# Rows turned between output halves, a second state buffer, and the first output weights converted behind three blocks' decayed scores of the last scan

## The chip, the cores and the metric

The kernel runs on one core of a Trainium2 chip. Its engines each have their own queue of instructions and run beside each other: TensorE (PE, with its weight loads PEld), VectorE (DVE), ScalarE (ACT), GpSimd (POOL) and SyncE (SP), whose queue issues most of the DMAs. The metric is device time in microseconds, the median of several executions. The profile records one execution in detail.

## The reference

One step of a hybrid diffusion backbone with one layer: 128 context tokens and 1024 latent tokens of width 1024. Each layer norms and modulates its input, projects it once, and feeds two groups of heads side by side: grouped-query attention (8 query heads of 64) and a bidirectional mLSTM (4 heads of 128), a scan over chunks of 128 tokens in both directions. Both are merged by one output projection, and a gated feed-forward net of width 2816 follows.

```python
def trunk_layer(x, mods, ...):
    h = rmsnorm(x, norm1_w) * (1 + sc1) + sh1
    aq, ak, av, mq, mk, mv, mo, mg = jnp.split(h @ w_in, SPLIT_POINTS, axis=-1)
    attn_o = attention(aq, keys, vals)
    hm, st_f, st_b = mlstm_bidir(heads(mq), heads(mk) * (MLSTM_DK ** -0.5), heads(mv), gates, init_f, init_b)
    hm = rmsnorm(hm.transpose(0, 2, 1, 3), mlstm_norm_w.reshape(MLSTM_HEADS, MLSTM_DV))
    hm = (hm.reshape(B, T, MLSTM_WIDTH) * jax.nn.sigmoid(mo.astype(F32))).astype(x.dtype)
    mix = jnp.concatenate([attn_o, hm], axis=-1) @ w_out
    x = x + g1 * mix
    h2 = rmsnorm(x, norm2_w) * (1 + sc2) + sh2
    x = x + g2 * swiglu(h2, w_gu, w_down)
```

Inside the scan, the step for one chunk:

```python
    s = jnp.einsum('bhld,bhsd->bhls', qc, kc) * jnp.exp(log_d - m_t[..., None])
    num = jnp.einsum('bhls,bhse->bhle', s, vc) + inter[..., None] * jnp.einsum('bhld,bhde->bhle', qc, C)
    h = num / jnp.maximum(jnp.abs(den), jnp.exp(-m_t))[..., None]
    C_new = decay[..., None, None] * C + jnp.einsum('bhs,bhsd,bhse->bhde', w, kc, vc)
```

## The kernel before

The 1152 tokens are nine blocks of 128 rows (block 0 is the context), in three groups of three. Products that need full precision are made from a high and a low part of each operand: ACT rounds a tile to its high part (a CAST, L157 for weights), DVE or POOL subtracts it from the full tile (L137) to get the low part, and PE makes three products, high by high, high by low and low by high. So each weight piece of 128x1024 costs one cast and one subtraction.

The order of the instructions on each engine is not written out by hand. The program is written as generators that are woven together, and the scheduler of the Tile framework places what they emit on the engines by its own timeline, within limits: `tc.high_priority` moves a piece forward, and `tc.issue_after(x)` places what follows behind instruction x in that order, without a semaphore of its own. Buffers come from pools with a tag and a count; a new tile of a tag waits until the oldest one has been read for the last time.

The stages that matter here:

The heads. `head_project(h)` makes the projections of mLSTM head h and, block by block, the state contributions; `head_mlstm(h)` is the scan of that head. Projection h runs woven with scan h - 1. Each head loads two initial states, forward (tag `c0f`, two buffers) and backward (tag `c0b`, one buffer): L807 and L808 on SP's queue. The states between blocks are tiles of tag `cs`, 21 buffers. The backward states are joined by seven steps in a row on DVE (L862), the first of which reads the backward initial state.

The last scan (head 3) has no projection beside it. For each block `weights(b)` makes a score product (L875), a decay in PSUM (L877, L878), two exponentials on ACT (`dt`, L881) and the decayed scores on DVE (`sd`, L883). Three blocks are made ahead. Then come the products with the states (L898), the evacuation `it` (L901), the products with the values (L905), and the normalisation on DVE, ACT and POOL. Beside this scan runs `attn_out_first`: the attention half of the output projection for blocks 0 to 2. It loads pieces of `w_out` into `ip` tiles, converts them to `ir` tiles (L157 on ACT, L137 on DVE), converts the attention output to `mxa` (L1310 on ACT, L137 on POOL) and makes twelve products for each block and each half of 512 columns (L1183 to L1185, here called output products). Products L364 for the remaining modulation also run there.

`prefill` comes next. It adds the mLSTM half of the output projection to the nine row blocks. For each block, `mix(b)` turns the block's 128 rows by four transposes (`hmr`, L116), casts them (`mx`, L1227) and subtracts (L137); `half(b, n)` makes twelve output products for one half of the columns and adds the gated result (DVE L1144, POOL L1145; for blocks 6 to 8 L1243 and L1244, with the row kept in DRAM); `end(b)` takes sums of squares (L1345) and starts the second norm (`y`, L1361). Blocks 0 and 1 are turned together ahead of the rest. Into this the attention of the second group of blocks is woven: for each head scores S on PE (L1075, one buffer of three PSUM banks), the row maximum on DVE (L1077), exponentials on ACT (`pr`, L1078), the scaled halves `ph` (ACT, L1081) and `pl` (DVE, L1082), transposes by DMA (L1084, L1085) and the products with the values (L1099, L1100).

Then the feed-forward net follows for the three groups, with gate and up products (L1382 to L1384) and down products (L1155 to L1157).

Of the kernel before, what the change touches and what calls it, by code (L numbers as in the profile page):

```python
# [8 lines left out]
F32 = mybir.dt.float32  # L9
# [4 lines left out]
AF = mybir.ActivationFunctionType  # L14
# [5 lines left out]
P = 128  # L20
# [17 lines left out]
LAST = [(0, 5), (5, 5), (10, 4), (14, 4), (18, 4)]  # L38
PAIRS = [(0, 1), (2, 3), (4,), (5, 6), (7, 8)]
NG = 4  # L40
CSB = 21
SINGLES = [(b,) for b in range(NB)]


# [1 line left out]
def hybrid_step(ctx: ExitStack, tc: tile.TileContext, I: dict, O: dict):  # L46
# [11 lines left out]
    def nm(s):  # L58
        uid[0] += 1
        return f"{s}_{uid[0]}"  # L60
# [57 lines left out]
    def bc(ap, axis, shape):  # L118
        return ap.unsqueeze(axis).to_broadcast(shape)
# [430 lines left out]
    for tag, shape, bufs, dt in (("hm", [P, NB, P], 2, F32), ("ssh", [P, NB], 2, F32), ("nu", [P, 2, P + 1], 4, F32), ("it", [P, 2, P + 1], 3, F32),  # L550
                                 ("dn", [P, 2], 3, F32), ("jkh", [P, P], 1, BF16), ("sd", [P, 2, P], 4, F32), ("dt", [P, 2, P], 4, F32),
                                 ("so", [P, P], 9, F32), ("va", [P, P + 1], 9, F32), ("kT", [P, P], 9, F32), ("th", [P, P], 1, F32),
                                 ("kt", [P, P], 2, F32), ("wv", [P, 2, P + 1], 2, F32), ("c0f", [P, P + 1], 2, F32), ("c0b", [P, P + 1], 1, F32),
                                 ("cs", [P, P + 1], CSB, F32), ("qTm", [P, CT], 2 * NCH, F32)):
        mlp.tile(shape, dt, name=f"lay_{tag}", tag=tag, bufs=bufs)

# [211 lines left out]
    def qcol(i, d, b, h):  # L768
        c = d * 64 + b * 4 + h
        return QT[:, i, c : c + 1]  # L770
# [3 lines left out]
    def head_project(h, st):  # L774
# [28 lines left out]
        st["s"] = states = {}  # L803
        st["raw"] = raws = {}
        for d in range(2):
            c0 = mlp.tile([P, P + 1], F32, name=nm("c0"), tag=("c0f", "c0b")[d], bufs=2 - d)
            dma(c0[:, 0:P], I["state_C"][0, 0, d, h])  # L807
            dma(c0[:, P : P + 1], I["state_n"][0, 0, d, h].rearrange("(p o) -> p o", o=1))  # L808
            states[d, 1 if d == 0 else NBL] = c0
# [47 lines left out]
    def head_mlstm(h, st):  # L857
# [14 lines left out]
        def weights(b):  # L872
            qTb = st["q"][b // CB][:, b % CB * P : (b % CB + 1) * P]
            pd = bank()
            mm(pd[:, 0:P], blocks[b][0], qTb, start=True, stop=True)  # L875
            r = b * 4 + h
            mm(pd[:, P : 3 * P], identb, maskb.rearrange("p d l -> p (d l)"), start=True, stop=False)  # L877
            mm(pd[:, P : 3 * P], selb[:, r : r + 1].to_broadcast([P, P]), NM3.rearrange("p d l -> p (d l)"), start=False, stop=True)  # L878
            dt = mlp.tile([P, 2, P], F32, name=nm("dt"), tag="dt", bufs=4)
            for d in range(2):  # L880
                act(dt[:, d], pd[:, (d + 1) * P : (d + 2) * P], AF.Exp, bias=qcol(0, d, b, h))  # L881
            sd = mlp.tile([P, 2, P], F32, name=nm("sd"), tag="sd", bufs=4)
            dve.tensor_tensor(out=sd, in0=bc(pd[:, 0:P], 1, [P, 2, P]), in1=dt, op=ALU.mult)  # L883
            return qTb, sd

        ahead = [weights(b) for b in range(depth)]
# [301 lines left out]
    def prefill(cur, nxt):  # L1188
# [16 lines left out]
        def load_x1(b):  # L1205
            if CB <= b < 2 * CB:
                dma(x1s[1][b % CB], xrow(b))
# [49 lines left out]
        for b in range(2):  # L1257
            half(b, 0)
            yield
        for b in range(2):  # L1260
            load_x1(b + 2)
            half(b, 1)
            yield
            yield from end(b)
        for b in range(2, NB):
            load_x1(b + 2)
            mix(b)
            yield
            for n in range(2):
                half(b, n)  # L1270
                yield
            yield from end(b)

    def attn_out_first(oT, ready):
# [18 lines left out]
        def out():  # L1293
            for n in range(2):
                cs = slice(n * 512, (n + 1) * 512)
                ws = []
                for j in range(2):
                    rows = w_out[2 * j * P : (2 * j + 2) * P, cs].rearrange("(a p) n -> p a n", p=P)
                    with tc.issue_after(sts[-1]["act"].ins), tc.issue_after(sts[-1]["dve"].ins):
                        ws.append(load_piece([(full_view, rows)], (2, 512), raw=raws[j], own=(his[j], los[j])))  # L1300
                for cnd in range(2):
                    dma(gt[:, 2 * n + cnd], g_d[0, cnd : cnd + 1, cs].to_broadcast([P, 512]))
                yield
                for i in range(CB):
                    while i not in ready:
                        yield
                    th, tl = mx[:, i, 0:4], mx[:, i, 4:8]
                    if n == 0:
                        dma(x1[:, i], xrow(i))
                        nc.scalar.copy(th, oT[i])  # L1310
                        sub(tl, oT[i], th.bitcast(F32), "pool")
                        yield
                    ps = out_block([ws], 0, th, tl)
                    v = x1[:, i, cs]
                    dve.tensor_tensor(out=gt[:, 4], in0=ps, in1=gt[:, 2 * n + (i > 0)], op=ALU.mult)
                    pool.tensor_tensor(out=v, in0=v, in1=gt[:, 4], op=ALU.add)
                    yield
# [310 lines left out]
```

## Time and profile before

| what | us |
|---|---|
| runs, median of 3 | 1536.48 |
| runs, lowest and highest | 1536.39, 1541.33 |
| profiled execution, its own time | 1540.57 |
| profiled execution, span from first to last instruction | 1538.8 |
| PE busy | 1479.7 |
| DVE busy | 1019.1 |
| ACT busy | 771.3 |
| POOL busy | 272.3 |

The last scan starts at about 446 us of the span, `prefill` at 490, and the first gate product of the feed-forward net at 577. From 600 to 880 us and from 920 to 1240, PE is shown busy all the time.

In a line of the timeline stand the start in us, the duration in us, the engine, the line of the kernel, the operation, the tiles written and read with their sizes, how many instructions are merged, and in brackets how long the engine idled before and what ended it. Matmuls overlap, so their durations add up to more than the time that they take. The clock is the share of full TensorE speed that was granted.

### The profile page before, as it was taken

The page shows a single profiled execution, that of the slowest core. Times are in us where ns is not written, and L with a number is a line of the kernel's source. Part 1 is how long each engine was busy: PE and PEld are TensorE (multiplying, and loading weights), DVE is VectorE, ACT ScalarE, POOL GpSimd, SP SyncE. Part 2 cuts the span into 40 slices and gives each one's busy share as a digit, 9 for nine tenths or more (in the row PEclk, how much of TensorE's full clock was granted, in tenths as well). Part 3 has the DMA queues.
Part 4 walks back from the last instruction along what each step waited for, and adds up shares of the span by engine and source line. Part 5 has one row for each costly group of instructions (what it writes and reads, how often), then busy time and mean ns, then how long its engine had stood idle before and what let it go on. Part 6 is the DMA issues. An engine that isn't in the chain of part 4 may idle for free.

```text
span 1538.8 us, 23409 instructions
## 1 busy us (share of the span) xinstructions
PE 1479.7 (96%) x8539; PEld 1245.3 (81%) x8539; DVE 1019.1 (66%) x2025; ACT 771.3 (50%) x1429; POOL 272.3 (18%) x354
## 2 busy tenths in 40 slices
PE   6799999999989899999999999999999999999997
PEld 3545567677766679899898989989898989999996
DVE  4878654838657875878646497887856584554554
ACT  4764475847654544555332445556553443333333
POOL 0112423233434441010010101000010101101110
PEclk9799999999999999999999999999999999999998
DMA  9664323523365566978634457877754445544441
GB/s 359 191 203 148 100 71 42 119 52 66 75 212 167 156 145 193 214 152 199 170 123 149 152 154 239 188 175 175 181 135 143 145 155 160 157 131 137 141 142 60
DMA packets 387113, 233.77 MB, mean 152 GB/s; under 512 B 170102, under 2 KB 347462, under 8 KB 386998
## 3 DMA queue, kind: packets, MB, share of 16 engines
q1 hardware_dynamic: 385006, 228.69, 54.0%
q10 hardware_dynamic: 1864, 3.20, 1.1%
q8 instruction: 67, 1.10, 0.3%
q14 instruction: 48, 0.39, 0.1%
q0 software_dynamic: 128, 0.39, 0.1%
HBM read 182.21 MB, written 11.69 MB: 126 GB/s over the span
## 4 chain that ended last, share of the span: by engine, by line
PE 58%; DVE 3%; DMA 1%; ACT 1%; issue 0%; ACTq 0%
PE mm L1383 12%; PE mm L1384 12%; PE mm L1382 12%; PE mm L1155 5%; PE mm L1156 5%; PE mm L1157 5%; PE S L1075 3%; PE po L1099 1%; PE po L1100 1%; PE mm L1185 1%; PE mm L1184 1%; PE mm L1183 1%; DVE fl L1371 1%; DVE wlo L137 1%; DVE t L1144 0%; DVE x L1145 0%
## 5 line engine op out<-in xcount | busy, mean ns | idle before, releaser
L157 ACT CAST whi<-raw 128x1024 fp32r<-128x1024 f32 (+1 forms) x216 | 221.8, 1027 | 390.3 <-PE mm L1383 151.5
L137 DVE TENSOR_TENSOR wlo<-raw,whi 128x1024 fp32r<-128x1024 f32 (+1 forms) x216 | 260.4, 1205 | 183.4 <-ACT whi L157 182.8
L1383 PE MATMUL mm<-aTl,whi 128*128 128x384 f32 x1056 | 355.9, 337 | 2.7 <-DVE aTl L137 2.7
L1384 PE MATMUL mm<-aTh,wlo 128*128 128x384 f32 x1056 | 354.1, 335 | 0.0
L1382 PE MATMUL mm<-aTh,whi 128*128 128x384 f32 x1056 | 352.5, 335 | 0.0
L137 POOL TENSOR_TENSOR hl<-tn,hl 128x384 fp32r<-128x384 f32 x66 | 85.3, 1292 | 848.7 <-ACT hl L1405 713.8
L1383 PEld LDWEIGHTS mm<-aTl,whi 128*128 128x128 f32 x1056 | 198.4, 188 | 3.9 <-DVE aTl L137 3.3
L1384 PEld LDWEIGHTS mm<-aTh,wlo 128*128 128x128 f32 x1056 | 198.4, 188 | 0.1
L1382 PEld LDWEIGHTS mm<-aTh,whi 128*128 128x128 f32 x1056 | 198.0, 188 | 0.6
L1156 PE MATMUL mm<-wlo,hl 128*128 128x512 f32 x372 | 145.3, 391 | 0.0
L1155 PE MATMUL mm<-whi,hl 128*128 128x512 f32 x372 | 144.1, 392 | 0.0
L1157 PE MATMUL mm<-whi,hl 128*128 128x512 f32 x372 | 142.6, 392 | 0.0
L1082 DVE SCALAR_TENSOR_TENSOR pl<-pr,st,ph 128x1152 f16<-128x1152 f32 (+1 forms) x72 | 96.0, 1334 | 33.0 <-ACT ph L1081 32.9
L1078 ACT ACTIVATE pr<-S,st 128x1152 f32<-128x1152 f32 (+1 forms) x72 | 81.2, 1128 | 34.5 <-DVE st L1077 33.9
L1077 DVE TENSOR_REDUCE st<-S 128x1 f32<-128x1152 f32 (+1 forms) x72 | 88.9, 1235 | 13.6 <-PE S L1075 12.9
L1081 ACT ACTIVATE ph<-pr,st 128x1152 f16<-128x1152 f32 (+1 forms) x72 | 83.8, 1164 | 20.9 <-DVE st L1080 8.0
L506 PE MATMUL wi<-headw,hT 128*128 128x384 f16 x288 | 93.9, 326 | 0.2 <-ACT th L792 0.2
L508 PE MATMUL wi<-headw,hT 128*128 128x384 f16 x288 | 93.9, 326 | 0.0
L507 PE MATMUL wi<-headw,hT 128*128 128x384 f16 x288 | 93.9, 326 | 0.0
L1144 DVE TENSOR_TENSOR t<-mm,gl 128x512 f32<-128x512 f32 x102 | 68.8, 685 | 27.5 <-DMA gl<-g_d 12.2
L1075 PE MATMUL S<-kst,qT 128*128 128x384 f32 (+1 forms) x400 | 84.4, 344 | 2.4 <-ACT pr L1078 2.4
L1157 PEld LDWEIGHTS mm<-whi,hl 128*128 128x128 f32 x372 | 69.9, 188 | 14.4
(396 smaller groups left out, 2647.7 us busy)
## 6 DMA issues: line engine op xcount, KB each, us to landing
raw<-in_w_gu_dram SPq DMA_DIRECT2D x132, 512.0 KB
raw<-in_w_down_dram SPq DMA_DIRECT2D x60, 512.0 KB
a<-in_w_ada_dram SPq DMA_DIRECT2D x24, 512.0 KB
gl<-g_d SPq DMA_DIRECT2D x36, 256.0 KB
aw<-in_w_ada_dram SPq DMA_DIRECT2D x16, 512.0 KB
iraw<-in_w_in_dram SPq DMA_DIRECT2D x32, 256.0 KB
raw<-in_w_out_dram SPq DMA_DIRECT2D x12, 512.0 KB
x<-in_x_sample_dram SPq DMA_DIRECT2D x11, 512.0 KB
```

The lines of the kernel that those rows point to most:

```text
L137: (dve if eng == "dve" else pool).tensor_tensor(out=out, in0=full, in1=hi, op=ALU.subtract)
L157: nc.scalar.copy(hi[:, :n], raw[:, :n])
L506: mm(ps[:, :n], ah, wh[:, k % 2, c0 : c0 + n], start=(k == 0), stop=False)
L507: mm(ps[:, :n], ah, wl[:, k % 2, c0 : c0 + n], start=False, stop=False)
L1075: mm(S[:, n, 0:w], qT[:, h, :], kst[kv][:, t, c0 + n * w : c0 + (n + 1) * w], start=(t == 0), stop=(t == 1))
L1082: dve.scalar_tensor_tensor(out=plv, in0=prv, scalar=st[:, 3:4], in1=phv, op0=ALU.mult, op1=ALU.subtract)
L1155: mm(ps, ah, wh[:, k % 2, :], start=(k == 0), stop=False)
L1156: mm(ps, ah, wl[:, k % 2, :], start=False, stop=False)
L1157: mm(ps, al, wh[:, k % 2, :], start=False, stop=(k == nk - 1))
L1382: mm(ps, wh[:, k, :], th[:, k, :], start=(k == 0), stop=False)
L1383: mm(ps, wh[:, k, :], tl[:, k, :], start=False, stop=False)
L1384: mm(ps, wl[:, k, :], th[:, k, :], start=False, stop=(k == KD - 1))
```

## The change

Three edits. The backward initial state gets a second buffer, and the chain of states one buffer less. In `prefill` a row block is turned between the two halves of the block before it (from block 2 on), where it was turned ahead of its own first half. And in `attn_out_first` the loading and conversion of each output weight piece is placed behind `dt` and `sd` of block 2 of the last scan.

```diff
-CSB = 21
+CSB = 20
...
-                                 ("kt", [P, P], 2, F32), ("wv", [P, 2, P + 1], 2, F32), ("c0f", [P, P + 1], 2, F32), ("c0b", [P, P + 1], 1, F32),
+                                 ("kt", [P, P], 2, F32), ("wv", [P, 2, P + 1], 2, F32), ("c0f", [P, P + 1], 2, F32), ("c0b", [P, P + 1], 2, F32),
...
-            c0 = mlp.tile([P, P + 1], F32, name=nm("c0"), tag=("c0f", "c0b")[d], bufs=2 - d)
+            c0 = mlp.tile([P, P + 1], F32, name=nm("c0"), tag=("c0f", "c0b")[d], bufs=2)
...
             for d in range(2):
-                act(dt[:, d], pd[:, (d + 1) * P : (d + 2) * P], AF.Exp, bias=qcol(0, d, b, h))
+                e = act(dt[:, d], pd[:, (d + 1) * P : (d + 2) * P], AF.Exp, bias=qcol(0, d, b, h))
             sd = mlp.tile([P, 2, P], F32, name=nm("sd"), tag="sd", bufs=4)
-            dve.tensor_tensor(out=sd, in0=bc(pd[:, 0:P], 1, [P, 2, P]), in1=dt, op=ALU.mult)
+            m = dve.tensor_tensor(out=sd, in0=bc(pd[:, 0:P], 1, [P, 2, P]), in1=dt, op=ALU.mult)
+            if alone and b == 2:
+                loaded["dt"], loaded["sd"] = e.ins, m.ins
...
-        for b in range(2):
-            load_x1(b + 2)
-            half(b, 1)
-            yield
-            yield from end(b)
+        load_x1(2)
+        half(0, 1)
+        yield
+        yield from end(0)
+        load_x1(3)
+        mix(2)
+        yield
+        half(1, 1)
+        yield
+        yield from end(1)
         for b in range(2, NB):
             load_x1(b + 2)
-            mix(b)
-            yield
-            for n in range(2):
-                half(b, n)
+            half(b, 0)
+            yield
+            if b + 1 < NB:
+                mix(b + 1)
                 yield
+            half(b, 1)
+            yield
             yield from end(b)
...
-                    with tc.issue_after(sts[-1]["act"].ins), tc.issue_after(sts[-1]["dve"].ins):
+                    with tc.issue_after(sts[-1]["act"].ins), tc.issue_after(sts[-1]["dve"].ins), behind("dt"), behind("sd"):
```

The scheduler makes a new order of this. In the changed kernel the lines behind the edits have moved: L1183 to L1185 are L1185 to L1187 there, L1310 is L1319.

ACT at the start of the last scan, before: the rows from the last block's key evacuation (`kT`) on. `ir` are the output weights' high parts, `mxa` the attention output's, `dt` the exponentials of blocks 0, 1, 2, ...

```order
L799 COPY kT_5717<-mm_5715 128x128
L157 CAST ir_5733<-ip_5731 128x1024
L828 COPY cs_5724<-mm_5722 128x129
L1310 CAST mxa<-oT_4936 128x512
L881 ACTIVATE dt_5753<-mm_5749,QT 128x128 x2
L157 CAST ir_5734<-ip_5732 128x1024
L881 ACTIVATE dt_5762<-mm_5758,QT 128x128 x2
L881 ACTIVATE dt_5771<-mm_5767,QT 128x128 x2
L881 ACTIVATE dt_5781<-mm_5777,QT 128x128 x2
```

The same place on ACT in the changed kernel:

```order
L799 COPY kT_5717<-mm_5715 128x128
L828 COPY cs_5724<-mm_5722 128x129
L1319 CAST mxa<-oT_4936 128x512
L881 ACTIVATE dt_5753<-mm_5749,QT 128x128 x2
L881 ACTIVATE dt_5762<-mm_5758,QT 128x128 x2
L881 ACTIVATE dt_5771<-mm_5767,QT 128x128 x2
L157 CAST ir_5733<-ip_5731 128x1024
L881 ACTIVATE dt_5781<-mm_5777,QT 128x128 x2
L157 CAST ir_5734<-ip_5732 128x1024
```

The first cast moved behind three blocks' exponentials, the second behind four.

PE in `prefill` around the second S, before: `y` are rows of the second norm, `hmr_6316` is row block 3, and `mx_6565` is that block turned and cast.

```order
L1185 MATMUL mm_6481<-whi_6293,mx_6455 128x512
L1075 MATMUL S_6501<-kst_1028,qT_6336 128x384 x6
L116 MATMUL mm_6540<-ident,y_6538 128x128 x4
L116 MATMUL mm_6553<-ident,y_6551 128x128 x4
L116 MATMUL mm_6566<-ident,hmr_6316 128x128 x4
L1183 MATMUL mm_6596<-whi_6269,mx_6565 128x512
L1184 MATMUL mm_6596<-wlo_6270,mx_6565 128x512
```

The turning of the same row block on PE in the changed kernel, where `mx_6398` is block 2:

```order
L1185 MATMUL mm_6465<-whi_6269,mx_6398 128x512
L1186 MATMUL mm_6465<-wlo_6270,mx_6398 128x512
L116 MATMUL mm_6482<-ident,hmr_6316 128x128 x4
L1187 MATMUL mm_6465<-whi_6269,mx_6398 128x512
L1185 MATMUL mm_6465<-whi_6269,mx_6398 128x512
```

The transposes of block 3 moved from right ahead of that block's own first product into the middle of block 2's first half.

SP's queue in `prefill`, before, from the first output weights (`raw`) on; `gx_all` and `gl` are gates, `x` the rows of the second group, and `raw` from `in_w_gu` the first pieces of the feed-forward net:

```order
L156 DMA raw_6268<-in_w_out_dram 128x2x512
L156 DMA raw_6274<-in_w_out_dram 128x2x512
L1213 DMA gx_all<-g_d 128x1024
L1198 DMA hmr_6306<-hm_d_78 128x512
L1175 DMA gl_6280<-g_d 128x512
L1175 DMA gl_6282<-g_d 128x512
L156 DMA raw_6286<-in_w_out_dram 128x2x512
L156 DMA raw_6292<-in_w_out_dram 128x2x512
L1200 DMA hmr_6316<-hm_d_79 128x4x128
L156 DMA raw_7057<-in_w_gu_dram 128x8x128
L156 DMA raw_7087<-in_w_gu_dram 128x8x128
L1207 DMA x_1234_6263<-in_x_sample_dram 128x1024 x3
```

And in the changed kernel:

```order
L156 DMA raw_6268<-in_w_out_dram 128x2x512
L156 DMA raw_6274<-in_w_out_dram 128x2x512
L1215 DMA gx_all<-g_d 128x1024
L1177 DMA gl_6280<-g_d 128x512
L1177 DMA gl_6282<-g_d 128x512
L1200 DMA hmr_6306<-hm_d_78 128x512
L1202 DMA hmr_6316<-hm_d_79 128x4x128
L156 DMA raw_6286<-in_w_out_dram 128x2x512
L156 DMA raw_6292<-in_w_out_dram 128x2x512
L1209 DMA x_1234_6263<-in_x_sample_dram 128x1024 x3
L156 DMA raw_7057<-in_w_gu_dram 128x8x128
L156 DMA raw_7087<-in_w_gu_dram 128x8x128
```

The three loads of `x` moved ahead of the first pieces of the feed-forward net, and block 3's rows ahead of the second half's output weights.

More of the change, by code (lines that the diff above doesn't have):

```diff
@@ L1259, in prefill @@
             yield
-        for b in range(2):
-            load_x1(b + 2)
+        load_x1(2)
[8 more added lines that the diff above has]
+        yield from end(1)
+        for b in range(2, NB):
+            load_x1(b + 2)
+            half(b, 0)
[3 more added lines that the diff above has]
+                yield
             half(b, 1)
             yield
-            yield from end(b)
-        for b in range(2, NB):
-            load_x1(b + 2)
-            mix(b)
-            yield
-            for n in range(2):
-                half(b, n)
-                yield
             yield from end(b)
```

## The prediction

> **What bounds the kernel now.** I read the page first: TensorE (PE) is busy 96% of the span, and the row of granted clock shows where it is not at speed.
>
> ```profile
> PE 1479.7 (96%) x8539; PEld 1245.3 (81%) x8539; DVE 1019.1 (66%) x2025; ACT 771.3 (50%) x1429; POOL 272.3 (18%) x354
> PEclk9799999999999999999999999999999999999998
> ```
>
> So time can only be had where PE idles or runs slow. Windows of 5 us (columns: time, then busy time and count of PE, PEld, DVE, ACT, POOL, the clock, the DMA share, GB/s) show such places in the stretch that the change touches:
>
> ```profile
> 450.00:455.00 5.00, 4.11 (x30) 2.63 (x31) 5.00 (x19) 0.62 (x2) 0.96 (x1) 0.68 0.54 183
> 490.00:495.00 5.00, 3.54 (x13) 2.32 (x12) 4.90 (x14) 4.08 (x11) 3.85 (x5) 0.77 0.90 271
> 495.00:500.00 5.00, 5.00 (x23) 3.97 (x23) 2.97 (x14) 1.53 (x2) 1.90 (x3) 0.88 0.79 250
> 500.00:505.00 5.00, 4.65 (x19) 3.19 (x18) 4.88 (x7) 1.63 (x2) 0.92 (x1) 1.00 0.82 250
> 515.00:520.00 5.00, 2.68 (x21) 2.37 (x19) 4.90 (x9) 1.69 (x4) 2.58 (x2) 1.00 0.71 147
> 520.00:525.00 5.00, 4.68 (x10) 3.27 (x11) 4.14 (x22) 5.00 (x9) 0.00 (x0) 0.50 0.07 19
> 525.00:530.00 5.00, 5.00 (x21) 4.12 (x20) 3.35 (x5) 0.23 (x1) 2.98 (x2) 0.81 0.40 77
> ```
>
> A slow clock costs busy time times (1 - clock): 4.11 x 0.32 = 1.3 us around 452, 0.8 + 0.6 = 1.4 around 495, 4.68 x 0.50 + 5.00 x 0.19 = 3.3 around 523. These are the places of three edits: the start of the last scan (446 to 456), the hand-over from the scan to the merged output rows (486 to 500), and those rows themselves (500 to 577). The timeline of PE names the waits there, in brackets the idle time and its releaser:
>
> ```profile
> 450.04 0.49 PE L875 MATMUL mm<-qT,kT 128*128 128x128 f32 x2 [2.42 <-DVE sd L883]
> 452.27 1.94 PE L364 MATMUL mm<-ip,gta 128*32 128x256 f32 x16 [0.85 <-DVE sd L883]
> 491.81 0.49 PE L1183 MATMUL mm<-whi,mx 128*128 128x512 f32 x1 [1.13 <-ACT mx L1227]
> 492.64 0.73 PE L1184 MATMUL mm<-wlo,mx 128*128 128x512 f32 x1 [0.33 <-DVE wlo L137]
> 502.59 0.50 PE L1184 MATMUL mm<-wlo,mx 128*128 128x512 f32 x1 [0.30 <-DVE wlo L137]
> 508.95 0.50 PE L1183 MATMUL mm<-whi,mx 128*128 128x512 f32 x1 [0.68 <-ACT mx L1227]
> 510.48 0.50 PE L1185 MATMUL mm<-whi,mx 128*128 128x512 f32 x1 [0.34 <-DVE rv L127]
> 519.99 0.77 PE L1183 MATMUL mm<-whi,mx 128*128 128x512 f32 x1 [2.32 <-ACT mx L1227]
> 521.50 0.80 PE L1185 MATMUL mm<-whi,mx 128*128 128x512 f32 x1 [0.32 <-DVE mx L137]
> 533.28 1.32 PE L1075 MATMUL S<-kst,qT 128*128 128x384 f32 x6 [1.64 <-ACT pr L1078]
> 546.74 0.50 PE L1185 MATMUL mm<-whi,mx 128*128 128x512 f32 x1 [0.91 <-DVE mx L137]
> 561.22 0.50 PE L1183 MATMUL mm<-whi,mx 128*128 128x512 f32 x1 [0.68 <-ACT mx L1227]
> ```
>
> Before the last scan PE's order is unchanged, and behind 577 only a few rows near 900 swap places; I count both at nothing, since PE stays the busy engine there.
>
> **Part A, start of the last scan.** Here PE makes the scores of four blocks into three PSUM banks; the fourth waits until DVE's sd of block 0 has emptied the first. What holds sd up:
>
> ```profile
> 441.58 0.56 SPq L808 DMA_DIRECT2D c<-in_state_n_dram  x1
> 445.65 1.04 ACT L157 CAST ir<-ip 128x1024 fp32r<-128x1024 f32 x1
> 447.45 1.62 POOL L137 TENSOR_TENSOR mxa<-oT,mxa 128x512 fp32r<-128x512 f32 x1 [1.09 <-ACT mxa L1310]
> 447.79 1.05 ACT L157 CAST ir<-ip 128x1024 fp32r<-128x1024 f32 x1
> 447.86 1.24 DVE L131 TENSOR_TENSOR rt<-ry 128x9 f32<-128x9 f32 x1
> 449.56 0.42 DVE L883 TENSOR_TENSOR sd<-mm,dt 128x256 f32<-128x256 f32 x1
> 451.79 0.42 DVE L883 TENSOR_TENSOR sd<-mm,dt 128x256 f32<-128x256 f32 x1
> ```
>
> The two weight casts take 2.09 us of ACT between the exponentials, their two subtractions (DVE) stand among the sd. The change puts the casts behind three exponentials, so sd of block 1, which ended at 451.79 + 0.42, can follow sd of block 0 after one or two small operations: some 1.5 us earlier, and the 0.85 us wait goes. The 2.42 us wait goes only in small part: a 128x9 product of DVE stood 1.24 us, until POOL's subtraction of mxa let it go at 449.07, and that subtraction now merely starts some 0.6 us earlier, with four steps of the state recurrence ahead of sd 0. I take 0.4 us there. The second state buffer lets the load that was issued at 441.58 go out a scan earlier; the recurrence waited for it only 0.2 us beyond POOL's lock, and its DMA, like those of the other heads, moves to places where SP's queue holds nothing that PE was seen to wait for: with cover, nothing; without it, a wait of the order of that 0.2. One state buffer fewer among 21 costs nothing as long as PE's order keeps old states ahead of new ones, as it does. The clock lost 1.3 us; with 2 us of waiting left I count half of it, 0.65. The casts come about as late as before, since ACT is free once the exponentials are done, and the first output products can start when the recurrence is through; there I take a further 0.1. Sum A: 0.85 + 0.4 + 0.65 + 0.1 = **2.0 us**. Bounds: all waits and clock gone, 2.42 + 0.85 + 1.3 = 4.6; first output products waiting for both subtractions, a loss of 1.5.
>
> **Part B, hand-over.** The first row blocks are still turned with nothing between, so the 1.13 us stays. Loading decides here:
>
> ```profile
> 483.20 0.82 SPq L1198 DMA_DIRECT2D hmr<-hm_d  x2
> 490.23 1.04 ACT L157 CAST whi<-raw 128x1024 fp32r<-128x1024 f32 x1
> 498.26 1.05 ACT L157 CAST whi<-raw 128x1024 fp32r<-128x1024 f32 x1 [4.18 <-DMA raw<-in_w_out_dram]
> ```
>
> The loads of hmr and of the output weights go out when the last product of the attention half is done (483.20), and in the new order PE has some scan products less behind that point and more ahead of it. So they start perhaps 1 us earlier, not 2, and the casts of whi now stand behind the two of mx: where the first was ready at 491.27, it now comes last, some 1 us of waiting more. I take **-0.5 us**, with bounds of -3 (a full cast and subtraction more on each of the two halves) and +2.9 (1.13 + 0.33 and the clock's 1.4 gone).
>
> **Part C, the rows.** Turning row b+1 now stands in the middle of row b, so that cast and subtraction have a half's twelve products as cover, from the first of them to the last:
>
> ```profile
> 519.37 0.56 ACT L1227 CAST mx<-mm 128x512 fp32r<-128x512 f32 x1
> 534.44 0.39 PE L1183 MATMUL mm<-whi,mx 128*128 128x512 f32 x1
> 536.93 0.39 PE L1185 MATMUL mm<-whi,mx 128*128 128x512 f32 x1
> ```
>
> That is 2.9 us against 0.56 for the cast and about as much on DVE. Waits named mx go: 0.68 + 0.34 + 2.32 + 0.32 + 0.91 + 0.68 = 5.25. The 1.64 us wait for S, two score products close behind each other, is spread, since a half and a turn now stand between them: 6.9 us in all. What is late next is the chain that feeds S and the normalised rows:
>
> ```profile
> 500.59 2.34 SPq L156 DMA_DIRECT2D raw<-in_w_gu_dram  x2
> 503.10 1.70 SPq L1207 DMA_DIRECT2D x<-in_x_sample_dram  x3
> 504.08 4.84 POOL L1145 TENSOR_TENSOR x1a<-x1a,t 128x512 f32<-128x512 f32 x3 [4.41 <-DVE t L1144]
> 505.48 1.05 ACT L157 CAST whi<-raw 128x1024 fp32r<-128x1024 f32 x1 [3.58 <-DMA raw<-in_w_gu_dram]
> 510.01 1.20 ACT L1078 ACTIVATE pr<-S,st 128x1152 f32<-128x1152 f32 x1
> 513.75 1.41 DVE L1082 SCALAR_TENSOR_TENSOR pl<-pr,st,ph 128x1152 f16<-128x1152 f32 x1
> ```
>
> POOL's gated additions take 1.6 us each, the sums of squares wait for them on ACT, and behind these stand pr, ph and the normalised y. Working forward with these durations, PE meets two waits of about 1 us, at the first y and at the third S: I count 2.0 us against the 6.9. Of the clock's 3.3 us I keep 2.4: a 1.13 us wait was followed by 1.4 us lost, a 1.64 us wait by none to speak of, so two of about 1 us may cost 0.9. Sum C: 6.9 - 2.0 + 2.4 = **7.3 us**, bounds 0 (new waits as long as the old) and 10.2 (none).
>
> The clock term is where the Trainium skill speaks against the change. "TensorE: Matmul & The Clock Gate", Part 1, says that the gate drops to half after an idle window of some 3.4 us. The longest wait here is 2.42 us, and still 0.50 was granted behind the 2.32 us wait, so the trace shows shorter gaps doing it, or another cause. By the page the slow stretches would not go with the waits, and the sum would be 3 us less.
>
> **Sum.** 2.0 - 0.5 + 7.3 = 8.8 us. The profiled execution took 1540.57 us with a span of 1538.8, 4.1 us above the median of 1536.48; the gain is taken off both: 1531.8 for a like execution, **1527.7 us** as a median.
>
> **Rivals.** (1) The attention chain takes over: S has one buffer, and ACT and DVE spent 1.2 and 1.41 us per head on pr and pl besides ph and the row maximum. For it: PE already waited for pr at 533.28. Against it: ACT is half idle. C shrinks to 1.5: 3.0 us in all, 1533.5.
> (2) The clock falls anyway, as part of a pattern that no single wait sets. For it: 1.64 us of waiting left the clock whole. Against it: each slow stretch begins at a wait. Without 2.4 and 0.65: 1530.8. The page of the Trainium skill named under part C would have it so.
> (3) The scan does not do what it says: POOL's lock simply stands ahead of sd. A is 0.4: 1529.3.
> (4) Slower: the three loads of x (1.5 MB) now stand ahead of the w_gu loads on SP, and ACT's cast of w_gu stands ahead of pr, of the sums of squares and of row 3's cast. At the 250 GB/s of the window 500 to 505, 1.5 MB are 6 us. If x starts no earlier than at 503.10, w_gu lands 6 us late, at about 511; then PE waits 6 us for pr and for row 3, loses some 3 us more at half clock, and the two score chains behind slip by 2: 8.8 - 11 gives 1538.7. It decides once w_gu lands later than about 510. Against it: x needs no buffer that PE was seen holding, so it should go out near 492.
> (5) More than forecast, no new waits: 1522.
>
> **How the numbers follow.** Chances: forecast 0.55, (1) 0.17, (2) 0.07, (3) 0.06, (4) 0.10, (5) 0.05. About 0.5%, 7.7 us, is what a measurement of this kernel can tell: faster means below 1528.8, slower above 1544.2. The forecast case spreads over 1523 to 1532 and lies below 1528.8 in 0.7 of it: 0.39; with (5) and a half of (3) and of (2): 0.51. Slower: half of (4) and a little: 0.06. Same: 0.43. The range runs from 1521, which holds most of (5), to 1537.5, which holds (1) to (3) and the better part of what lies between them and (4).
>
> **What would show it.** A: PE's wait for the first sd stays near 2 us, the second is gone, and the casts of ir stand behind three exponentials. B: hmr issues near 482, and the first output products still wait a microsecond or more. C: no wait named mx above 0.5 us, clock 1.00 in most windows between 510 and 535, new waits at y or S of about 1 us, and gate and up products starting near 568 instead of 577. I am wrong if PE waits at S or po more than 4 us in all, if ACT's cast of the first w_gu piece ends after 510, or if the time won by 577 is gone again at 920.

## The result, and the profile after

| | before | changed |
|---|---|---|
| runs | 22 | 22 |
| median, us | 1539.45 | 1535.37 |
| lowest and highest | 1536.29, 1541.8 | 1533.14, 1538.82 |
| profiled execution, own time | 1540.57 | 1537.59 |
| profiled execution, span | 1538.8 | 1535.8 |

The ratio is 0.9977, 95% interval 0.997 to 0.9984: the change is worth 3.5 us (2.5 to 4.6), where 8.8 were forecast. That is within 0.5% of before, and outside what the forecast case held. The median of before, now of 22 runs, is 3.0 us above the three runs from which 1527.7 was worked out; the gain does not depend on that.

The page of the changed kernel has nearly the same first line (PE 3.9 us less, POOL 5.5 us less), and a row of granted clock that differs in its last digit alone; the place of the gain can't be read from it:

```profile
PE 1475.8 (96%) x8539; PEld 1243.1 (81%) x8539; DVE 1018.8 (66%) x2025; ACT 772.4 (50%) x1429; POOL 266.8 (17%) x354
PEclk9799999999999999999999999999999999999999
```

To compare the executions part by part I use marks on PE that stand in both: the last but one state contribution ahead of the last scan (L817), the first transposes of hmr, the first transposes of qr, and the first S behind the second of these. Of before, from PE's timeline:

```profile
442.12 0.68 PE L817 MATMUL mm<-wv,kt 128*128 128x258 f32 x2
489.59 1.09 PE L116 MATMUL mm<-ident,hmr 128*128 128x128 f32 x8 [0.59 <-DVE nu L908]
496.98 0.60 PE L116 MATMUL mm<-ident,qr 128*128 128x128 f32 x4
607.35 1.21 PE L1075 MATMUL S<-kst,qT 128*128 128x384 f32 x6
```

Of the changed kernel, with PE's waits of 0.4 us and more between the marks (lines of the kernel are 2 higher behind the scan's new lines, 9 higher behind `prefill`):

```profile
441.02 0.67 PE L817 MATMUL mm<-wv,kt 128*128 128x258 f32 x2
444.85 0.49 PE L875 MATMUL mm<-qT,kT 128*128 128x128 f32 x2 [0.64 <-ACT kT L799]
448.29 0.49 PE L875 MATMUL mm<-qT,kT 128*128 128x128 f32 x2 [1.86 <-DVE sd L883]
463.50 1.02 PE L473 MATMUL mm<-hmx,strip_sel 128*2 128x512 f32 x2 [1.61 <-ACT hmx L464]
484.94 1.32 PE L116 MATMUL mm<-ident,hmr 128*128 128x128 f32 x8
490.49 0.80 PE L1185 MATMUL mm<-whi,mx 128*128 128x512 f32 x1 [4.23 <-ACT whi L157]
491.75 0.80 PE L1186 MATMUL mm<-wlo,mx 128*128 128x512 f32 x1 [0.46 <-DVE wlo L137]
496.07 0.60 PE L116 MATMUL mm<-ident,qr 128*128 128x128 f32 x4
502.14 0.50 PE L1186 MATMUL mm<-wlo,mx 128*128 128x512 f32 x1 [0.47 <-DVE wlo L137]
516.45 1.27 PE L116 MATMUL mm<-ident,y 128*128 128x128 f32 x8 [2.10 <-ACT y L1370]
528.55 0.50 PE L1185 MATMUL mm<-whi,mx 128*128 128x512 f32 x1 [2.98 <-DVE mx L137]
545.47 0.47 PE L1185 MATMUL mm<-whi,mx 128*128 128x512 f32 x1 [0.90 <-DVE fl L1380]
584.84 0.27 PE L1102 MATMUL po<-plT,vs 128*128 128x256 f16 x1 [1.18 <-DMA plT<-pl]
604.15 1.32 PE L1077 MATMUL S<-kst,qT 128*128 128x384 f32 x6
```

1.10 us of the 3 us between the two spans are there already at the first mark, ahead of which PE's order is the same; I put them down to the two executions (`behind_only` below, whose only edit acts later, has the mark at 438.32 us). Behind it the terms of the prediction read as follows, in us from mark to mark.

| term | before | changed | gained | forecast |
|---|---|---|---|---|
| A, L817 to hmr | 47.47 | 43.92 | 3.55 | 2.0 |
| B, hmr to qr | 7.39 | 11.13 | -3.74 | -0.5 |
| C, qr to the S mark | 110.37 | 108.08 | 2.29 | 7.3 |
| sum | 165.23 | 163.13 | 2.10 | 8.8 |

Behind the last mark nothing more is won or lost: 607.35 - 604.15 = 3.2 there, 3.0 at the ends of the spans. In the windows of 5 us the clock is whole from 440 to 485, where 1.3 us had been lost around 452, but not at the hand-over nor behind the wait for mx:

```profile
485.00:490.00 5.00, 1.20 (x8) 0.74 (x8) 3.60 (x13) 2.73 (x9) 0.91 (x2) 0.86 0.89 243
490.00:495.00 5.00, 4.04 (x9) 2.87 (x10) 3.64 (x11) 1.49 (x2) 0.50 (x1) 0.50 1.04 372
530.00:535.00 5.00, 5.00 (x23) 3.80 (x22) 2.35 (x4) 3.06 (x4) 1.50 (x2) 0.70 0.15 32
```

So the scan's gain is given back at the hand-over, in a wait of 4.23 us and 4.04 x 0.50 = 2.0 us of half clock, and the rows wait nearly as long as before: 0.47 + 2.10 + 2.98 + 0.90 + 1.18 = 7.6 us, against the 8.0 of before (the 6.9 that the prediction counted, 0.30 for wlo, and 0.82 at po near 588). Of the 2.29 us of C the waits are thus 0.4; most of the rest is the clock, which lost 3.3 us there before and about 5.00 x 0.30 = 1.5 now.

Why the hand-over holds the gain is seen on SP and ACT. From PE's timeline the last output product of the attention half, from SP's the loads, from ACT's the first cast:

```profile
481.67 0.39 PE L1187 MATMUL mm<-ir,mxa 128*128 128x512 f32 x1
482.09 0.82 SPq L1200 DMA_DIRECT2D hmr<-hm_d  x2
483.01 0.90 SPq L156 DMA_DIRECT2D raw<-in_w_out_dram  x2
489.40 1.04 ACT L157 CAST whi<-raw 128x1024 fp32r<-128x1024 f32 x1 [1.09 <-DMA raw<-in_w_out_dram]
```

The loads go out with that product, 482.09 - 441.02 = 41.07 us behind the first mark; before it was 483.20 - 442.12 = 41.08. PE has 14 of the scan's products more ahead of this product than before (56 for 42 into `wi`, counted in the two traces), and fewer behind it. So what the scan won lies behind this product and not ahead of it, and the loads start no earlier.

### The profile page after: what moved, and what is told of

Its sections match the earlier page's. It is cut to its first block, busy times and chain, and to the rows that moved or that the text cites. A ratio compares the mean times of both kernels' runs of the same rounds, so it can differ in the third digit from the quotient of the medians.

```text
span 1535.8 us, 23413 instructions
## 1 busy us (share of the span) xinstructions
PE 1475.8 (96%) x8539; PEld 1243.1 (81%) x8539; DVE 1018.8 (66%) x2025; ACT 772.4 (50%) x1429; POOL 266.8 (17%) x354
## 4 chain that ended last, share of the span: by engine, by line
PE 59%; DVE 3%; DMA 1%; ACT 1%; issue 0%; POOL 0%; SPq 0%; ACTq 0%
PE mm L1392 11%; PE mm L1393 11%; PE mm L1391 11%; PE mm L1157 5%; PE mm L1158 5%; PE mm L1159 5%; PE S L1077 3%; PE po L1102 1%; PE po L1101 1%; PE mm L1185 1%; PE mm L1187 1%; PE mm L1186 1%; DMA raw<-in_w_gu_dram 1%; DVE fl L1380 1%; DVE wlo L137 1%; DVE t L1146 1%
## 5 line engine op out<-in xcount | busy, mean ns | idle before, releaser
L1146 DVE TENSOR_TENSOR t<-mm,gl 128x512 f32<-128x512 f32 x102 | 68.7, 684 | 28.5 <-DMA gl<-g_d 13.1
L1159 PEld LDWEIGHTS mm<-whi,hl 128*128 128x128 f32 x372 | 69.9, 188 | 14.4
```

Of the source, the lines that this page charges most:

```text
L1159: mm(ps, al, wh[:, k % 2, :], start=False, stop=(k == nk - 1))
```

## The experiments

Each ratio is to the kernel before, from runs on the same chip; 0.001 is 1.54 us. The marks of all traces stand in one table further down.

**The parts alone.** Theory L says that the hand-over swallows the scan's gain; its rival S, that the scan brought the 3.5 us.

`rows_only`, the kernel before with the loop of `prefill` alone:

```diff
         for b in range(2, NB):
             load_x1(b + 2)
-            mix(b)
+            half(b, 0)
...
+                mix(b + 1)
...
+            half(b, 1)
```

> The kernel before with the turning of the rows alone. Theory L (the hand-over is bound by the load of the output weights, which goes out with the last product of the attention half; so nothing that the scan wins gets past it, and the whole of the measured 3.5 us comes from the rows): 2.5 to 4 us faster, ratio near 0.998, rows shorter by some 2 to 4 us between the first output product (491.8) and the products of gate and up, and a wait of 2 to 3 us for mx or y stays inside them. Rival S (the scan gives the 3.5 us, the rows nothing): no change, ratio 1.000.

Measured 0.9968 (0.9955 to 0.9981): 4.9 us faster, somewhat more than L expected, and S has it at nothing. A wait for the attention chain stays, longer than the 1.64 us of before. PE's timeline:

```profile
515.97 2.29 PE L1075 MATMUL S<-kst,qT 128*128 128x384 f32 x6 [3.12 <-ACT pr L1078]
```

`state_only`, the second buffer and CSB 20:

```diff
-tag=("c0f", "c0b")[d], bufs=2 - d)
+tag=("c0f", "c0b")[d], bufs=2)
```

> The kernel before with the second buffer for the backward start state, and 20 in place of 21 buffers for later states. Only SP's order differs, each start-state load one head earlier. Every theory: within 0.5 us of before. If this alone gives 1 us or more, or costs it, the term that I counted at nothing was wrong.

Measured 0.9991 (0.998 to 1.0001): no difference that can be told; hmr comes no earlier (48.35 us behind the mark, 47.47 before). `behind_only`, the ordering without the buffer:

```diff
-with tc.issue_after(sts[-1]["act"].ins), tc.issue_after(sts[-1]["dve"].ins):
+with tc.issue_after(sts[-1]["act"].ins), tc.issue_after(sts[-1]["dve"].ins), behind("dt"), behind("sd"):
```

> The kernel before with the weights' load and casts ordered behind the third block's exponential and decayed scores, one state buffer as before. Theory L: the scan is done 2 to 4 us earlier at the transposes of hmr, the wait for whi at the first output product grows by as much (to 3 to 4 us, with half clock behind it), and the time is within 1 us of before. Rival S: 3 to 4 us faster, ratio 0.998.

Measured 0.9995 (0.9984 to 1.0006). As much as L expected of the time, but not for its reason: the scan was not done earlier (48.14 us behind the mark). PE now waited 3.54 us for the first sd, since the recurrence ahead of it on DVE stood for the backward state, whose load went out at the head's start. Single lines from PE's, SP's and DVE's timeline of `behind_only`, then from DVE's of the changed kernel:

```profile
446.99 0.79 PE L875 MATMUL mm<-qT,kT 128*128 128x128 f32 x2 [3.54 <-DVE sd L883]
438.27 0.67 SPq L808 DMA_DIRECT2D c<-in_state_n_dram  x1
445.78 0.35 DVE L862 SCALAR_TENSOR_TENSOR cs<-c,decb,cs 128x129 f32<-128x129 f32 x1 [2.60 <-DMA c<-in_state_n_dram]
```

```profile
445.36 0.35 DVE L862 SCALAR_TENSOR_TENSOR cs<-c,decb,cs 128x129 f32<-128x129 f32 x1
```

`scan_only` has both of these edits, and the rows as before.

> Both edits of the scan, rows as before. Theory L: as the ordering alone, within 1 us of before, last product of the attention half near 482 to 483 and first output product 8.4 to 8.6 us behind it. Rival S: 3 to 4 us faster. A third, that the rows depend on how early the scan ends (the whole change is more than its parts): both halves alone give nothing.

Measured 1.0011 (0.9999 to 1.0023), 1.7 us slower (-0.2 to 3.5): rival S falls, and with the rows' 4.9 us faster the two parts add up to 3.2, close to the 3.5 of the whole. With the buffer the scan is done 43.88 us behind the mark, and the first output product still comes at 49.49, as L has it. The rows even take longer than before, which no theory expected by so much. ACT's and SP's timeline:

```profile
505.15 1.04 ACT L157 CAST whi<-raw 128x1024 fp32r<-128x1024 f32 x1 [6.27 <-DMA raw<-in_w_gu_dram]
...
497.03 1.29 SPq L1209 DMA_DIRECT2D x<-in_x_sample_dram  x3
498.43 2.09 SPq L156 DMA_DIRECT2D raw<-in_w_gu_dram  x2
```

ACT stands 6.27 us for w_gu, whose loads were put behind the three of x. In the order of before they stand ahead of x.

**The load at the hand-over, and the subtraction on POOL.** `early_out`: the changed kernel with the first two output-weight loads ahead of hmr and their buffers in another place.

```diff
-        his, los, raws = ir[0:2], ir[2:4], ip[2:4]
+        his, los, raws = ir[0:2], ir[2:4], ip[0:2]
...
-            return ip[turn[0] % 2].rearrange("p (k n) -> p k n", k=4)
+            return ip[2 + turn[0] % 2].rearrange("p (k n) -> p k n", k=4)
...
     wp = ctx.enter_context(tc.tile_pool(name="wp", bufs=1, reuse_waits="tile"))
+    wp.tile([P, 1024], F32R, name="lay_whi", tag="whi", bufs=4)
...
-        hms = [load_hm(0), load_hm(1)]
         ws = [out_pieces(1, 0)]
+        hms = [load_hm(0), load_hm(1)]
```

> The changed kernel, with the first output-weight loads ahead of hmr on SP and their buffers laid over memory that is free some 20 us earlier. Theory L (the hand-over is bound by that load): the loads go out before the last product of the attention half, the 4.23 us wait for whi shrinks to about 2 (cast and subtraction of mx), the half clock behind it goes, and the time is 2 to 4 us below the changed kernel, ratio to before 0.995 to 0.9965. Rival R (the rows end with the attention chain, whenever they start): same as the changed kernel, 0.9977, with the won time lost again at S, y or mx before the last S of the rows.

Measured 0.9937 (0.9925 to 0.995): 6 us below the changed kernel. More than L expected, and rival R, no gain, falls; but it was not won where L expected it: the wait moved to hmr (2.94 us), the first output product comes only 1 us earlier, and 6 us were won in the rows. The loads had moved by 2.5 us only (39.46 us behind the mark, against 41.99): SP waited up to 10.1 us for an output product (L1187) to free that place. `rows_early` is the same without the edits of the scan.

> The kernel before with the turning of the rows and with the early output-weight loads, without the edits of the scan. Theory L: there the hand-over waits for mx (1.09), so the load is nearly hidden: at most 1.6 us below the rows alone (waits for wlo of 0.37, 0.57 and 0.69 go), ratio to before 0.9955 to 0.9968. Rival: as much won as with the scan edits, 2 to 4 us, ratio 0.9945 to 0.9955.

Measured 0.9964 (0.9951 to 0.9977), no more than the rows alone, as L has it. `sub_on_dve` is the changed kernel with aTl subtracted on DVE:

```diff
-sub(tl[:, half * 4 : half * 4 + 4, i * P : (i + 1) * P], full, oh.bitcast(F32), "pool" if c == 0 else "dve")
+sub(tl[:, half * 4 : half * 4 + 4, i * P : (i + 1) * P], full, oh.bitcast(F32), "dve")
```

> The changed kernel, with the subtractions of the normalised rows (aTl) on DVE in place of POOL. Theory P (the 2.98 us wait for mx comes from pl standing 2.49 instead of 1.41 us on DVE while POOL subtracts aTl): pl at 1.41, that wait about 1 us shorter, 1 to 2 us faster than the changed kernel, ratio to before near 0.997. Rival D (DVE is the full queue there, ten subtractions of 0.69 us more on it cost as much or more): no faster than the changed kernel, 0.9977 or above.

Measured 0.9962 (0.995 to 0.9974). The place is this, lines of DVE and then POOL of the changed kernel:

```profile
525.40 2.49 DVE L1084 SCALAR_TENSOR_TENSOR pl<-pr,st,ph 128x1152 f16<-128x1152 f32 x1
527.82 0.68 DVE L137 TENSOR_TENSOR mx<-mm,mx 128x512 fp32r<-128x512 f32 x1
524.18 2.50 POOL L137 TENSOR_TENSOR aTl<-fl,aTh 128x512 fp32r<-128x512 f32 x2 [1.19 <-ACT aTh L1385]
```

and DVE and PE of `sub_on_dve`:

```profile
524.95 1.41 DVE L1084 SCALAR_TENSOR_TENSOR pl<-pr,st,ph 128x1152 f16<-128x1152 f32 x1
526.27 0.68 DVE L137 TENSOR_TENSOR mx<-mm,mx 128x512 fp32r<-128x512 f32 x1
527.01 0.50 PE L1185 MATMUL mm<-whi,mx 128*128 128x512 f32 x1 [1.42 <-DVE mx L137]
```

pl took 2.49 us beside POOL's subtractions and 1.41 without them, and the wait fell from 2.98 to 1.42: the mechanism of this wait is shown. That is what "SBUF — State Buffer" of the Trainium skill, under "Who interferes with whom", says of a DVE instruction with two inputs in SBUF beside a POOL instruction that reads SBUF; the trace agrees, with 2.49 us against 1.41. Its worth is not certain: the interval overlaps that of the changed kernel. `rows_sub`, the rows alone with the same edit:

> The kernel before with the turning of the rows and the subtractions of aTl on DVE. Theory P: the 3.12 us wait for pr at the third S shrinks by about 1 us, ratio to before 0.996 to 0.9965 (rows alone 0.9968). Rival D: 0.9968 or above.

Measured 0.9973 (0.9964 to 0.9981): nothing won, and the 3.12 us wait for pr is the same as in `rows_only`. Rival D holds there.

**When the load goes out, with one and the same order.** `swap_only` has only the last piece of `early_out`'s diff, `early2` all but the line `lay_whi`. On every engine the three have the same instructions in the same order; they differ in when the buffers come free.

> The changed kernel with the first two output-weight loads ahead of hmr on SP and nothing else; every engine has the order of the run early_out, but the buffers lie where the conditioning weights lay, free some 3 us earlier than there. Theory O (early_out won by the order of the rows on ACT and DVE that came with the swap, not by when the load went out): ratio 0.993 to 0.995, as early_out. Theory L (the load sets the hand-over): the wait for hmr of 2.94 us falls below 1.5 and the half clock behind it goes, 1 to 3 us below early_out, 0.9915 to 0.993.

> The same order once more, with the buffers laid over the staging of the attention half's own output weights, free 10 to 15 us before hmr can be loaded. Theory O: as early_out, 0.993 to 0.995. Theory L: both pieces are there before PE is, the hand-over then waits for hmr and the cast of mx alone; 1.5 to 3.5 us below early_out, ratio 0.991 to 0.993.

Measured 0.9946 (0.9934 to 0.9959) and 0.9948 (0.9935 to 0.996), like `early_out`, as theory O has it. The loads went out 34.54 and 33.81 us behind the mark, 7 to 8 us earlier than in the changed kernel, and the first output product came when it had come before. So theory L is right that the gain of the scan ends at the hand-over, and wrong that the load alone holds it: with the load that much earlier nothing is won there. Lines from the timelines of SP, ACT and PE in `swap_only`:

```profile
474.34 0.88 SPq L156 DMA_DIRECT2D raw<-in_w_out_dram  x2
486.54 1.03 ACT L157 CAST whi<-raw 128x1024 fp32r<-128x1024 f32 x1
488.71 1.06 ACT L1229 CAST mx<-mm 128x512 fp32r<-128x512 f32 x2
489.34 0.79 PE L1185 MATMUL mm<-whi,mx 128*128 128x512 f32 x1 [3.68 <-ACT mx L1229]
```

With the load out of the way ACT's order takes its place, by the trace: both casts of whi stand behind the last head's normalisation, and the cast of mx behind these. No run moved these casts alone. `scan_swap` puts the swap on `scan_only`:

> The two edits of the scan and the swapped loads, with the rows as before the change. Theory L: what the scan wins can now pass the hand-over, 3 to 5 us below scan_only, ratio 0.9975 to 0.999. Theory O: the rows keep their old order and their old waits for mx, no more than 1.5 us below scan_only, 1.000 or above.

Measured 0.9979 (0.997 to 0.9988), 4.9 us below `scan_only`, the amount that L expected; but again not at the hand-over. There the swap put one w_gu load ahead of x, and ACT's cast of it came at 499.12 instead of 505.15:

```profile
499.12 1.06 ACT L157 CAST whi<-raw 128x1024 fp32r<-128x1024 f32 x1 [1.31 <-DMA raw<-in_w_gu_dram]
```

`early2_sub` is `early2` with aTl on DVE:

> As early2, and the subtractions of aTl on DVE in place of POOL. If the gain of sub_on_dve (2.3 us under the changed kernel) is one of POOL holding up pl, it adds to the other: 1 to 2.5 us below early2. If it came from a place that the swap has emptied already: no faster than early2, or slower by the ten subtractions that DVE takes over.

Measured 0.9964 (0.9952 to 0.9976): not faster than `early2`, so that gain doesn't add to the swap's.

The marks, each worked out as above from PE's timeline of the run, in us behind the first mark; "rows" is from qr to the S mark, the last column the cast of the first w_gu piece behind the first output product.

| run | hmr | first output product | rows | w_gu cast | ratio |
|---|---|---|---|---|---|
| before | 47.47 | 49.69 | 110.4 | 13.7 | 1 |
| changed | 43.92 | 49.47 | 108.1 | 16.8 | 0.9977 |
| rows_only | 47.96 | 50.14 | 106.2 | 13.4 | 0.9968 |
| state_only | 48.35 | 50.53 | 110.3 | 14.3 | 0.9991 |
| behind_only | 48.14 | 51.16 | 109.2 | 13.7 | 0.9995 |
| scan_only | 43.88 | 49.49 | 113.9 | 17.5 | 1.0011 |
| sub_on_dve | 43.49 | 48.74 | 105.1 | 17.0 | 0.9962 |
| rows_early | 47.43 | 49.94 | 106.5 | 14.2 | 0.9964 |
| rows_sub | 47.26 | 49.68 | 107.4 | 14.4 | 0.9973 |
| scan_swap | 44.10 | 49.01 | 108.7 | 10.9 | 0.9979 |
| early_out | 46.65 | 48.48 | 102.0 | 13.1 | 0.9937 |
| swap_only | 44.61 | 49.54 | 100.9 | 11.3 | 0.9946 |
| early2 | 43.91 | 48.81 | 101.7 | 10.7 | 0.9948 |
| early2_sub | 43.47 | 48.48 | 103.0 | 10.6 | 0.9964 |
| late_x | 44.51 | 50.86 | 107.5 | 12.1 | 0.9962 |
| scan_late_x | 44.17 | 50.37 | 112.9 | 14.5 | 0.9997 |
| swap_late_x | 44.10 | 49.04 | 101.8 | 10.4 | 0.994 |

The first output product comes 48.5 to 51.2 us behind the mark in all of them, whether PE is done with the scan at 43.5 or at 48.4.

**The loads of x.** The swap won in the rows; the most visible thing that it did there was to put a w_gu load ahead of x. To move x, a column of its buffer is written behind the cast of row 2's turn, so that the three loads have to wait for it (the column is overwritten by the load). The scheduler answers with a changed order on PE, ACT and DVE too, so x is not all that moves:

```diff
             nc.scalar.copy(th, psv)
+            if b == 2:
+                for x in x1s[1]:
+                    nc.scalar.copy(x[:, 0:1], ps[:, 0:1])
+                for x in range(CB, 2 * CB):
+                    load_x1(x)
             sub(tl, psv, th.bitcast(F32), "dve")
...
-        load_x1(2)
...
-        load_x1(3)
...
-            load_x1(b + 2)
```

> The changed kernel with the three loads of x (rows 3 to 5) made to wait, by a copy of one column into their buffer behind the cast of row 2's turn, so that they go out behind the first loads of w_gu; the hand-over is left as it is (3 to 4 us of waiting for whi). Theory X (with the scan edits the loads of x stand ahead of w_gu, the cast of w_gu comes 17 us behind the first output product where it came 11 to 14 before, and pr, sums of squares and the next turns slip behind it on ACT): the cast of w_gu 10 to 14 us behind the first output product, 3 to 6 us below the changed kernel, ratio to before 0.9935 to 0.996. Rival H (the swap won at the hand-over): as the changed kernel, 0.9965 to 0.9985.

> The two edits of the scan with the rows as before, and the same late loads of x. Theory X: the 6.27 us that ACT stood for w_gu in scan_only go, 3 to 5 us below scan_only, ratio 0.9975 to 0.9992. Rival H: as scan_only, 1.000 to 1.002.

> Swapped loads and late x together. Theory X: the swap had already put a w_gu load ahead of x, so within 1.5 us of the swap alone, 0.9935 to 0.9955. Rival H (two causes, at the hand-over and at x): both gains, 0.990 to 0.993.

Measured 0.9962 (0.995 to 0.9975), 0.9997 (0.9987 to 1.0007) and 0.994 (0.9927 to 0.9953). The cast of w_gu came earlier, as theory X has it (12.1, 14.5 and 10.4 us behind the first output product). On the changed kernel and on `scan_only` that is worth some 2.2 us by the ratios, each hardly clear of noise, between what X and its rival H expected; by the marks the rows are only 0.6 and 1.0 us shorter. With the swap it adds nothing that can be told. The swap wins 4.8 and 4.9 us there. So the loads of x are not shown to be more than a part of the loss.

What came in their place can be read on ACT. In `scan_late_x`, with w_gu there in time, ACT stands for POOL's gated addition instead, since the sum of squares `jk` is ahead of the cast of mx in its queue:

```profile
504.74 1.06 ACT L157 CAST whi<-raw 128x1024 fp32r<-128x1024 f32 x1 [2.35 <-DMA raw<-in_w_gu_dram]
509.51 1.06 ACT L1350 ACTIVATE jk<-x1a 128x1024 bf16<-128x1024 f32 x1 [3.71 <-POOL x1a L1147]
510.68 0.59 ACT L1229 CAST mx<-mm 128x512 fp32r<-128x512 f32 x1
```

This cast comes 20.4 us behind the first output product, and 19.6 in `scan_only`; before, where it stood ahead of `jk` on ACT, 16.5. So the late loads of x exchanged one wait on ACT for another: x1a was later too, as on DVE the subtraction for the early w_gu piece (505.83 to 507.53 us) stood ahead of the product `t` that x1a is made from. In `late_x` ACT waits 2.76 us for x1a at the same place. Which part of the order of ACT and DVE the swap mends, the runs do not tell; `late_x` still waits 2.79 us at the first y, `swap_only` 0.99.

## Why the prediction was wrong

The steps, in its own order.

**A, start of the scan.** The mechanism was right: the wait for the first sd stayed (1.86 us, "near 2 us" forecast), the second went, and the clock of this place was whole. The size was too small, 3.55 for 2.0, in spite of a new wait of 1.61 us for hmx. The step that failed in it is the state buffer, counted at nothing because "the recurrence waited for it only 0.2 us beyond POOL's lock". That was how late it was behind the conversions; with these out of the way it is 2.60 us late. Each edit alone brings hmr no further forward (48.35 and 48.14 us behind the mark, 47.47 before); together they bring it to 43.9, and the time is still no better (1.0011).

**B, the hand-over.** This is the first failing step: "I take **-0.5 us**". The prediction had read that the loads go out with the attention half's last product, and that this moves by 1 us at most; but it added A to B as if the scan's gain went through. PE's time to the first output product was set by the load, and behind it, as far as the trace of `swap_only` tells, by ACT's order, not by the end of the scan: the product moved by 0.2 us against the mark, for hmr's 3.55. A and B together are -0.2, where +1.5 was forecast, and the scan's two edits without the rows measure 1.7 us slower (-0.2 to 3.5).

**C, the rows.** The second failing step: "PE meets two waits of about 1 us". It set 2.0 us of new waits against 6.9 of old ones; PE met 7.6 against 8.0. The waits named mx did go in part (5.25 before, of which 0.34 were for rv and not for mx; 2.98 now), and the waits for S are gone; what came is 2.10 at y and 2.98 at mx, beside some smaller ones. Both stand behind pl in DVE's queue: the third turn's subtraction behind the pl of 2.49 us, and y, by DVE's and ACT's timeline of the changed kernel, for an `ry` behind the pl before it:

```profile
514.16 1.41 DVE L1084 SCALAR_TENSOR_TENSOR pl<-pr,st,ph 128x1152 f16<-128x1152 f32 x1
515.49 0.15 DVE L133 SCALAR_TENSOR_TENSOR ry<-rt,ry 128x1 f32<-128x1 f32 x1
515.67 1.33 ACT L1370 ACTIVATE y<-x1a,ry 128x512 f32<-128x512 f32 x2 [2.62 <-DVE ry L133]
```

In `swap_only`, where PE waits 0.99 us for y, no pl stands there. That is read from the traces; only the second pl was taken out of the way by a run (`sub_on_dve`). The clock term, 2.4, was nearer: 3.3 - 1.5 = 1.8. Alone, the rows' edit is worth 4.9 us (2.9 to 6.9), so 7.3 was too much by half. On top of the scan's edits it is worth about the same, 5.2 (1.0011 to 0.9977); C shows only 2.29 in the table because the scan's edits lengthen the rows (113.9 us in `scan_only`, 110.4 before), a cost that the prediction does not have as a term.

**The rivals.** (1), 1533.5, came nearest in time: 3.0 us. Its mechanism, the chain for S, did not come as it was told: no wait for S or pr is left in the changed kernel, and of the chain only pl on DVE is in the way, ahead of y and mx. In `rows_only` it is there, 3.12 us for pr. So the nearness is in part luck. (4) happened in part: x goes out ahead of w_gu, at 498.96 and not near 492, and ACT's cast of w_gu slips from 13.7 to 16.8 us behind the first output product. In the changed kernel, though, that cast waits for no load; it stands behind a sum of squares that waits 1.95 us for x1a. Its point of decision, a landing later than 510, was not reached (the cast ran at 507.25), and its price was 11 us where `late_x` shows about 2, hardly clear of noise. (2), the clock, is taken up below. (3) and (5) fall: A moved, and the waits came.

**The signs.** The three conditions that would have shown the forecast wrong (4 us at S or po, the w_gu cast behind 510, time lost again at 920) did not come true; it was wrong all the same, as none of them asked for the hand-over. Of the signs that it was right, those of A came, and the clock was whole in three of the five windows from 510 to 535; "no wait named mx above 0.5 us" failed, with 2.98. Gate and up products start at 572.94, 4.1 us earlier, of which 1.1 belong to the execution, not at 568.

**A version that beats both.** The changed kernel with two lines of `prefill` swapped (`swap_only`) is at 0.9946 of before, 8.3 us faster (6.3 to 10.2); `early_out` and `swap_late_x`, with the same swap, are at 0.9937 and 0.994.

## What to carry to other kernels

Before two gains are added, find for each the event that the next stage starts from: a gain that ends behind that event (here the last product that frees the buffers of the next weights) is handed back at the seam as a new wait, however real it is. Where a scheduler sets the order, two edits of one place may each leave a stage where it was and move it only together, as the two of the scan did, and may change the order of loads elsewhere; test them apart and together, and look at the order of the large loads behind the edit first. And when a load that held a stage is made early, look at what stands in the queue of the engine that consumes it, since that is the next bound.

## What the hardware showed that was not expected

The same wait need not cost the same clock. `state_only` has PE's order of before; PE's timeline and the windows show the same wait for mx and the same share of work around it, and no slow clock behind it:

```profile
519.57 0.50 PE L1183 MATMUL mm<-whi,mx 128*128 128x512 f32 x1 [2.29 <-ACT mx L1227]
...
515.00:520.00 5.00, 2.71 (x20) 2.29 (x18) 4.83 (x11) 2.11 (x4) 2.16 (x2) 1.00 0.49 113
520.00:525.00 5.00, 4.22 (x19) 3.23 (x18) 4.86 (x22) 4.81 (x9) 0.40 (x1) 1.00 0.00 0
```

Before, 2.32 us of waiting were followed by 0.50 and 0.81, a loss of 3.3 us; here 2.29 us were followed by 1.00. So the clock terms of the prediction, 0.65 and 2.4 us, were read from one execution and need not repeat, and a difference of 1 to 3 us between two profiles can be that alone; the terms A, B and C above carry this uncertainty, the ratios do not. "TensorE: Matmul & The Clock Gate" of the Trainium skill, Part 1, says that the activity window is free-running, so that the result depends on where in it the work falls. These two traces are in keeping with that; the 3.4 us that the page gives for an idle window do not fit so well, since the 2.32 us of before were followed by a slow clock.
